# Where tiles start in SBUF: moving whole-row tiles from 128 bytes past a multiple of 256 to multiples of 1 KiB

## The chip, the cores and the metric

The kernel runs on one core of one Trainium2 chip; the program uses none of the others. The metric is the device time of one execution in microseconds (us), median of several.

## The reference, cut to what matters

`x` has the shape 8 x 4096 x 2112, float32, 276.8 MB. Each group of four consecutive rows has its mean taken off:

```python
x_r = x.reshape(B, S // 4, 4, D)
pooled = x_r.mean(axis=2)
upsampled = np.repeat(pooled, 4, axis=1)
return (x - upsampled).astype(np.float32)
```

Every byte has to be read from HBM once and written once; the page has 276.82 MB read and 276.82 MB written.

## The kernel before

One group of four rows is 8448 floats, 33792 bytes, and is put into one partition; 128 groups make a tile of 4.3 MB. There are 64 tiles. They lie in SBUF, the core's own memory; `x` and the output lie in HBM, the large memory. A load goes from HBM to SBUF, a store back. Loads are issued from the sync queue, stores from the scalar queue, and six buffers let them overlap.

```python
STRIDE = 4
IO_BUFS = 6
...
    W = STRIDE * D                                              # 8448
    xg = x.rearrange("b (g f) d -> (b g) (f d)", f=STRIDE)      # 8192 x 8448
    og = out.rearrange("b (g f) d -> (b g) (f d)", f=STRIDE)

    io_pool = ctx.enter_context(tc.tile_pool(name="io", bufs=IO_BUFS))
    sum_pool = ctx.enter_context(tc.tile_pool(name="sum", bufs=1))

    for g0 in range(0, G, P):
        gsz = min(P, G - g0)
        x_tile = io_pool.tile([P, W], mybir.dt.float32)
        nc.sync.dma_start(out=x_tile[:gsz], in_=xg[g0:g0 + gsz])          # load
        ...                                    # three tensor_add: s = sum of the four rows
        nc.vector.scalar_tensor_tensor(...)    # x_tile = s * (-1/4) + x_tile
        nc.scalar.dma_start(out=og[g0:g0 + gsz], in_=x_tile[:gsz])        # store
```

In the built program the first `x_tile` starts at byte 16512 of each partition, which is 64 x 256 + 128. A buffer is 33792 = 132 x 256 = 33 x 1024 bytes long, so all six start 128 bytes past a multiple of 256.

## Time and profile before

The median is 1286.44 us. What matters of the profile (a packet is one record of a DMA engine in the trace; a row packet moves one partition's 33792 bytes):

| what | value | view |
|---|---|---|
| span | 1284.7 us | page |
| VectorE (DVE) busy | 1026.1 us, 80% | page, busy times |
| DMA engines busy | 9 tenths or more in 39 of 40 slices | page, slices |
| loads and stores, share of the 16 engines' span | 50.0% and 49.9% | page, DMA queues |
| DVE waiting for loads | 237.3 us | waits |
| a row packet of 33792 bytes, recorded duration | 1251 ns, median of both queues | packet records in the trace |

These are lines of the page of the kernel before. "q1" carries the loads and "q10" the stores (packets, MB, share of 16 engines' span). In the slices each digit is the busy share of a fortieth of the span in tenths. In the groups of instructions the columns are: line, engine, operation, tiles, shapes, count, then busy us, mean ns of one, and idle time just before.

```profile
span 1284.7 us, 674 instructions
DVE 1026.1 (80%) x256; POOL 0.2 (0%) x4
...
DVE  5998778787787877878778787787887878778784
...
DMA  9999999999999999999999999999999999999998
...
q1 hardware_dynamic: 9216, 276.83, 50.0%
q10 hardware_dynamic: 9216, 276.83, 49.9%
...
L46 DVE SCALAR_TENSOR_TENSOR x_tile<-s,x_tile 128x8448 f32<-128x8448 f32 x64 | 573.3, 8958 | 2.2
L43 DVE TENSOR_TENSOR s<-x_tile 128x2112 f32<-128x2112 f32 x64 | 150.9, 2358 | 237.5 <-DMA x_tile<-in_x_dram 237.3
L45 DVE TENSOR_TENSOR s<-s,x_tile 128x2112 f32<-128x2112 f32 x128 | 301.8, 2358 | 4.4
```

The two queue shares add up to the whole span: the DMA engines have no slack. DVE has 20%, and it lies just where DVE waits for a load. The stretches view (busy times, granted clock, DMA share, GB/s) says the same of a short stretch and of the long middle:

```profile
core 0: us, DVE busy (x) POOL busy (x), PEclk, DMA share, GB/s
8.00:30.00 22.00, 16.81 (x5) 0.00 (x0) 1.00 1.00 433
100.00:1200.00 1100.00, 881.46 (x221) 0.00 (x0) 1.00 1.00 433
```

433 GB/s is the steady rate.

### The profile page before, as it was taken

Reading aid. Unit: us, or ns where it says so; the run is one execution under the profiler, and the core shown is the slowest. Engines: PE = TensorE matmul, PEld = TensorE weight load, DVE = VectorE, ACT = ScalarE, POOL = GpSimd, SP = SyncE. Lnnn points to the kernel's source line nnn. Section 1 sums busy time; section 2 is a strip of 40 time slices with the busy share of each in tenths; the row PEclk is TensorE's granted clock in tenths of the full one; section 3 lists DMA queues with packets and bytes.
Section 4 is the critical chain, followed back from the end, with each engine's and each line's share of the span. In section 5 each row is a group of like instructions: output and inputs, shape, how many; then the busy total and the mean of one; then the engine's idle time right before and its main releaser. Section 6 shows DMA issues by size and latency. Waiting matters only on the chain.

```text
span 1284.7 us, 674 instructions
## 1 busy us (share of the span) xinstructions
DVE 1026.1 (80%) x256; POOL 0.2 (0%) x4
## 2 busy tenths in 40 slices
DVE  5998778787787877878778787787887878778784
POOL 0000000000000000000000000000000000000000
DMA  9999999999999999999999999999999999999998
GB/s 404 421 438 438 433 425 437 438 427 432 437 437 426 435 437 431 429 437 437 431 428 438 437 431 429 437 436 432 428 438 436 430 430 437 437 426 433 438 431 380
DMA packets 18437, 553.70 MB, mean 431 GB/s; under 512 B 2048, under 2 KB 2048, under 8 KB 2048
## 3 DMA queue, kind: packets, MB, share of 16 engines
q1 hardware_dynamic: 9216, 276.83, 50.0%
q10 hardware_dynamic: 9216, 276.83, 49.9%
q14 instruction: 5, 0.04, 0.0%
HBM read 276.82 MB, written 276.82 MB: 431 GB/s over the span
## 4 chain that ended last, share of the span: by engine, by line
DVE 80%; another core or an unknown queue 17%; DMA 1%; issue 1%; DVEq 0%
DVE x_tile L46 45%; DVE s L45 24%; DVE s L43 12%; DMA x_tile<-in_x_dram 1%; DVEq L43 0%
## 5 line engine op out<-in xcount | busy, mean ns | idle before, releaser
L46 DVE SCALAR_TENSOR_TENSOR x_tile<-s,x_tile 128x8448 f32<-128x8448 f32 x64 | 573.3, 8958 | 2.2
L43 DVE TENSOR_TENSOR s<-x_tile 128x2112 f32<-128x2112 f32 x64 | 150.9, 2358 | 237.5 <-DMA x_tile<-in_x_dram 237.3
L45 DVE TENSOR_TENSOR s<-s,x_tile 128x2112 f32<-128x2112 f32 x128 | 301.8, 2358 | 4.4
L69 POOL MEMSET const-bfloat16-1.0<- 128x1 bf16 x1 | 0.1, 103 | 0.0
L69 POOL MEMSET const-uint8-127<- 128x1 uint8 x1 | 0.1, 102 | 0.0
L69 POOL MEMSET const-float32-0.0<- 128x1 f32 x1 | 0.1, 100 | 0.2 <-issue 0.2
L69 POOL MEMSET const-float32-1.0<- 128x1 f32 x1 | 0.1, 99 | 0.0
## 6 DMA issues: line engine op xcount, KB each, us to landing
x_tile<-in_x_dram SPq DMA_DIRECT2D x64, 4224.0 KB, 59.6
out_dram<-x_tile ACTq DMA_DIRECT2D x64, 4224.0 KB, 43.8
```

Source lines behind the costliest of these rows:

```text
L43: nc.vector.tensor_add(out=s[:gsz], in0=rows[:, 0, :], in1=rows[:, 1, :])
L45: nc.vector.tensor_add(out=s[:gsz], in0=s[:gsz], in1=rows[:, f, :])
L46: nc.vector.scalar_tensor_tensor(out=rows, in0=s[:gsz, None, :].to_broadcast([gsz, STRIDE, D]), scalar=-1.0 / STRIDE, in1=rows, op0=mybir. ...
L69: nc = _bacc.Bacc("TRN2", target_bir_lowering=False, num_devices=1)
```

## The change

The intent is to have every row start at an SBUF address that is a multiple of 1 KiB. That a start 128 bytes past a multiple of 256 costs each packet the time of 128 bytes (4 beats), 4.8 us in all, was the author's guess; no trace had shown it. A small tile that nobody uses is allocated first:

```diff
+PAD = 224
...
+    pad_pool = ctx.enter_context(tc.tile_pool(name="pad", bufs=1))
+    pad_pool.tile([P, PAD], mybir.dt.float32, name="pad")
     io_pool = ctx.enter_context(tc.tile_pool(name="io", bufs=IO_BUFS))
```

The 896 bytes move the first tile from 16512 to 17408 = 17 x 1024, and the other five with it. The instructions and their order on each engine stay the same. Here and in the recorded texts a beat is 32 bytes and a cycle 1.176 ns, the time of 32 bytes by the measured difference between packets of 33792 and of 768 bytes (1214.0 ns for 33024 bytes, at run768_aligned below). Both are units for reckoning; no run shows a clock or steps of that size. In these units the bytes of a row are 1056, and its recorded 1251 ns are 1063, 7 more.

## The prediction

> **What bounds the kernel now.** The DMA engines. The page shows a span of 1284.7 us, DVE busy 1026.1 us (80%), and DMA at 9 tenths in all but the last slice; the queue table gives the loads 50.0% and the stores 49.9% of the 16 engines' span. Each moves 276.83 MB as 8192 row packets of 33792 bytes (one partition row of a tile) and 1024 small ones. Share times span times 16 over 8192 gives 1.25 us a packet; the trace's packet records say it sharply: the median packet of either queue takes 1251 ns. An engine serves 2 x 8192 / 16 = 1024 row packets one after another: 1024 x 1.251 = 1281.0 us, leaving 5.4 us of the measured 1286.44 for start, end and a few slow packets. DVE's only large wait is 237.3 us for loads (the wait table). The chain of waits is 80% DVE work, but runs through queues that are never empty: DVE has 20% slack, DMA none.
>
> **What the change does.** It adds an unused 896-byte tile, so that the first x tile moves from byte 16512 of a partition (64 x 256 + 128) to 17408 (17 x 1024). A tile row is 33792 = 132 x 256 bytes, so all six buffers keep that alignment, and HBM rows keep theirs. The instruction order is the same. DVE operands move together and should keep their 8958 and 2358 ns.
>
> **What it is worth.** [...] All of it is critical: the engines are never idle. 1286.4 - 4.8 = 1281.6 us, 0.4%.
>
> The doubt: [...] a load writes SBUF and reads an HBM row that is aligned already. Yet load packets take the same 1251 ns. Either a write pays too, or the 7 cycles over 1056 are all fixed, and nothing is gained. I give the full gain 60%, stores alone 10%, nothing 25%. [...]
>
> **Predicted:** 1281.8 us, range 1279.5 to 1286.8 (8 in 10). Faster by over 2%: 0.02; within 2%: 0.97; slower: 0.01.
>
> **What would show it.** Median row packet of both queues 1246 ns in place of 1251 (1251 for loads only: writes don't pay; for both: no effect). Steady slices' GB/s up by about 0.4% (mean from 431 to 432 or 433). DVE's groups unchanged, its idle time before the first add 237 us down by about 5. DMA still at 9 tenths throughout.
>
> **What would make it wrong.** A fixed overhead instead of the 4 beats; another cost of alignment[...].

## The result, and the profile after

In the same rounds the kernel after took 1286.45 us (median of 6 runs, 1286.41 to 1286.58) and the kernel before 1286.48 us (6 runs, 1286.44 to 1287.14). The ratio is 0.9999, with a 95% interval of 0.9986 to 1.0012. Here and below a ratio is the mean time of one kernel's fast runs over the mean of the other's fast runs of the same rounds, so it is not quite the ratio of the medians. The 4.8 us that I gave a 60% chance did not come.

The lines of the page after that answer to those above:

```profile
span 1284.8 us, 674 instructions
DVE 1026.1 (80%) x256; POOL 0.2 (0%) x4
...
q1 hardware_dynamic: 9216, 276.83, 50.0%
q10 hardware_dynamic: 9216, 276.83, 49.9%
...
L49 DVE SCALAR_TENSOR_TENSOR x_tile<-s,x_tile 128x8448 f32<-128x8448 f32 x64 | 573.3, 8958 | 2.2
L46 DVE TENSOR_TENSOR s<-x_tile 128x2112 f32<-128x2112 f32 x64 | 150.9, 2358 | 237.6 <-DMA x_tile<-in_x_dram 237.3
L48 DVE TENSOR_TENSOR s<-s,x_tile 128x2112 f32<-128x2112 f32 x128 | 301.8, 2358 | 4.4
```

And the stretches view of the kernel after:

```profile
8.00:30.00 22.00, 16.74 (x5) 0.00 (x0) 1.00 1.00 432
100.00:1200.00 1100.00, 881.52 (x221) 0.00 (x0) 1.00 1.00 433
```

The same DVE durations, the same wait of 237.3 us, the same rate. The packet records agree: the median row packet takes 1251 ns in both queues, before and after.

One thing in the packet records is different from what I had read before. The *duration* of a packet is not its *pace*. I sorted the starts of the row packets between 200 and 1100 us and took every sixteenth, since 16 engines run side by side. The difference from one to the next is 1247 ns in 635 of 721 cases before and in 635 of 720 after, and 1247.9 ns on average in both (the average contains what the small packets cost: the page counts 2048 under 512 bytes, 16 for each of the 128 transfers). So recorded packets of one engine overlap by about 4 ns, and an engine finishes a row every 1247 ns, not every 1251. Of the 1286.4 us, 1024 x 1247.9 ns = 1277.8 us are rows, and some 8.6 us start and end. 1247 ns are 1060 cycles: the 1056 of the bytes and 4 more.

### The profile page after: what moved, and what is told of

It reads as the page before. It is cut to its first block, busy times and chain, and to the rows that moved or that the text cites. A ratio compares the mean times of both kernels' runs of the same rounds, so it can differ in the third digit from the quotient of the medians.

```text
span 1284.8 us, 674 instructions
## 1 busy us (share of the span) xinstructions
DVE 1026.1 (80%) x256; POOL 0.2 (0%) x4
## 2 busy tenths in 40 slices
DMA packets 18437, 553.70 MB, mean 431 GB/s; under 512 B 2048, under 2 KB 2048, under 8 KB 2048
## 4 chain that ended last, share of the span: by engine, by line
DVE 80%; another core or an unknown queue 17%; DMA 1%; issue 1%; DVEq 0%
DVE x_tile L49 45%; DVE s L48 24%; DVE s L46 12%; DMA x_tile<-in_x_dram 1%; DVEq L46 0%
## 5 line engine op out<-in xcount | busy, mean ns | idle before, releaser
L46 DVE TENSOR_TENSOR s<-x_tile 128x2112 f32<-128x2112 f32 x64 | 150.9, 2358 | 237.6 <-DMA x_tile<-in_x_dram 237.3
```

The lines of the kernel that those rows point to most:

```text
L46: nc.vector.tensor_add(out=s[:gsz], in0=rows[:, 0, :], in1=rows[:, 1, :])
```

## The experiments

Twelve kernels ran, in three calls. "Pace" is always the mean distance of packet starts on one engine (all starts in a stretch, times 16), from the packet records; the stretches view shows the same as GB/s. Three stretches are told apart in each run: the first 30 us or so, when only loads run because no tile is ready to be stored; the long middle, where loads and stores alternate (before, 32 loads and 32 stores start in each 5 us once the mix is steady); and the last 30 us or so, stores alone.

### First call: does a start off 256 cost anything at all?

To make a cost per packet large, rows are cut into runs of 768 bytes, 3 blocks of 256, each placed at its own 1 KiB step in SBUF. HBM stays contiguous. The results are still right.

```diff
-IO_BUFS = 6
+IO_BUFS = 4
+C = 192       # elements in one run of a row
+PITCH = 256   # elements from run to run in SBUF
+OFF = 0       # elements skipped before a run; 32 in run768_off128, 1 in run768_off4
...
-        x_tile = io_pool.tile([P, W], mybir.dt.float32)
-        nc.sync.dma_start(out=x_tile[:gsz], in_=xg[g0:g0 + gsz])
+        x_tile = io_pool.tile([P, W // C, PITCH], mybir.dt.float32)
+        data = x_tile[:gsz, :, OFF:OFF + C]
+        nc.sync.dma_start(out=data, in_=xg[g0:g0 + gsz].rearrange("p (n c) -> p n c", c=C))
...
```

The sums and the subtraction work on views of the same runs, one subtraction for each of the four rows; the pad of the change is kept, so that `OFF` alone sets the alignment.

The fourth kernel of the call is the kernel before with whole rows at 4 bytes past a multiple of 256:

```diff
+SKIP = 33   # from 128 bytes past a multiple of 256 to 4 bytes past one
...
-        x_tile = io_pool.tile([P, W], mybir.dt.float32)
+        x_wide = io_pool.tile([P, W + 64], mybir.dt.float32)
+        x_tile = x_wide[:, SKIP:SKIP + W]
```

**row_off4**

> Whole-row packets of 33792 bytes that start 4 bytes past a multiple of 256 in SBUF (before: 128 past; after: 0 past). Theory A, the start of a packet costs nothing and the 7 cycles over 1056 beats are paid at every address: row packets 1251 ns, time 1286.4 us. [...]

Measured: 1286.79 us, ratio to before 1.0002 (0.9986 to 1.0019); pace 1247 ns, median duration 1251 ns. Correct. A start 4 bytes past, which is not even a multiple of 32, costs nothing here either. (The later runs show that a mix hides a cost that one-way traffic has, 32.96 ns in the mix against 37.63 with loads alone for 768 bytes at 128 past, so this run says nothing of one-way traffic.)

**run768_aligned**

> Each row in 44 runs of 768 bytes, 1 KiB apart in SBUF, each at a multiple of 1 KiB; 45056 packets on an engine. It measures what a packet costs besides its bytes. [...] If instead the 1251 ns of a row is all rate (27.0 bytes a ns) and no packet overhead: 28.4 ns, about 1285 us. [...] it is the base of the next two.

Measured: 1494.05 us. The pace is 32.96 ns in the middle, more than the 28.4 ns expected without an overhead, and less than 7 cycles over the 24 beats would make it (31 cycles, 36.5 ns): my 7 cycles came from the recorded duration (36 ns here), not from the pace. From 768 to 33792 bytes the pace rises by 1247.0 - 32.96 = 1214.0 ns for 33024 bytes, which is 32 bytes in 1.1764 ns, or 27.2 bytes a ns on one engine: the cycle defined above. What remains of the 32.96 ns after 24 beats is 4.7 ns, 4 cycles. So the pace of both sizes is *bytes / 32 + 4* cycles a packet: 28 for 768 bytes, 1060 for a row.

The stretches view of run768_aligned shows loads alone, the mix, and stores alone, in this order:

```profile
10.00:30.00 20.00, 14.76 (x7) 0.00 (x0) 1.00 1.09 373
200.00:1200.00 1000.00, 698.17 (x301) 0.00 (x0) 1.00 1.09 373
1479.00:1487.00 8.00, 0.00 (x0) 0.00 (x0) 1.00 1.09 373
```

The DMA share of 1.09 is the overlap of recorded packets again (36 over 32.96 is 1.09). 373 GB/s throughout: aligned, the three stretches are alike.

**run768_off128**

> As run768_aligned, but each run starts 128 bytes past a multiple of 256 in SBUF. Theory A: same packet time and same total as run768_aligned within 1%. Theory B [...]: 4 beats more, 4.7 ns a packet, about 212 us more in all. [...]

Measured: 1499.68 us, 5.6 us or 0.4% more than run768_aligned, not 212. By its total theory A holds. But the same view says something else:

```profile
10.00:30.00 20.00, 12.72 (x6) 0.00 (x0) 1.00 1.09 326
200.00:1200.00 1000.00, 698.25 (x302) 0.00 (x0) 1.00 1.09 373
1484.00:1492.00 8.00, 0.00 (x0) 0.00 (x0) 1.00 1.04 327
```

With loads alone the rate is 326 in place of 373 GB/s, with stores alone 327; in the mix it is 373 as if the tiles were aligned. In the packet records the loads' pace is 37.63 ns against 32.95, exactly 32 cycles against 28. So an extra of the size in theory B, 4 cycles (4.7 ns), is there for these packets where traffic goes one way, and it vanishes where loads and stores alternate. Neither A nor B had this; the run was worth more by its stretches than by its time.

**run768_off4**

> As run768_aligned, but each run starts 4 bytes past a multiple of 256 in SBUF. Theory A: same as run768_aligned within 1%. Theory B: [...] 1 to 2 beats, 1.2 to 2.4 ns a packet, 50 to 110 us more. [...]

Measured: 1499.64 us, the same as run768_off128 within 0.04 us; 326 GB/s (37.65 ns, 32 cycles) with loads alone, 326 with stores alone, 373 in the mix. By its total theory A holds here too. 4 bytes and 128 bytes past cost the same, 4.7 ns more than aligned with loads alone, and not the 1.2 to 2.4 of theory B. What both runs share is that their 768 bytes touch four blocks of 256 bytes instead of three: four times 8 cycles (9.4 ns) is the 32 that both show.

### Second call: blocks or starts, and why is the mix spared?

The new theories are guesses from the paces of the first call: D (the cost belongs to an engine's reading or writing side and is averaged over loads and stores), E (it goes with the blocks touched in SBUF, and shows only while traffic goes one way), F (any start off 256 costs a fixed amount, whatever it touches). The first expectation has what each says in numbers.

Runs of 1408 bytes, 5.5 blocks, tell blocks from starts: 128 bytes past, they still touch 6 blocks; 192 bytes past, 7. The diff to run768_aligned:

```diff
-C = 192       # elements in one run of a row
-PITCH = 256   # elements from run to run in SBUF
+C = 352       # elements in one run of a row
+PITCH = 512   # elements from run to run in SBUF
-OFF = 0
+OFF = 0       # 32 in run1408_off128, 48 in run1408_off192
```

**run1408_off0**

> Each row in 24 runs of 1408 bytes (5.5 blocks of 256), 2 KiB apart in SBUF, at multiples of 2 KiB; 24576 packets on an engine. Theory D (sides): an engine spends beats + 4 cycles on a packet itself, and each of its two sides, the reading and the writing one, 8 cycles for each 256-byte block that the packet touches there; [...] over alternating loads and stores each side's mean counts, and the slowest of the three sets the pace. Here 44 + 4 = 48, sides 6 x 8 = 48: 48 cycles, 56.5 ns, about 1397 us. Theory E[...]: 48 cycles, 1397 us. Theory F (start): a side pays a fixed 8 cycles for any start off 256, not by blocks; half of the HBM runs start 128 past 256, so at the HBM side about 48 cycles as well: 1397 us.

Measured: 1398.90 us, pace 56.5 ns with loads alone and in the mix. The 4 cycles over the bytes are found at a third size: 44 + 4 = 48 cycles are 56.5 ns. (In the built program the runs start at 17408, which is 1 KiB past a multiple of 2 KiB, and not at multiples of 2 KiB; what the argument needs, a multiple of 256, holds.)

**run1408_off128**

> As run1408_off0, each run 128 bytes past a multiple of 256 in SBUF; it still touches 6 blocks. Theory D: no cost anywhere, 48 cycles in the loads-only start too, about 1397 us. Theory E with blocks: the same. Theory F: 52 cycles (61.2 ns) while only loads run, and in the mix (52 + 48) / 2 = 50 cycles, about 1455 us.

Measured: 1399.06 us; 56.46 ns with loads alone, 56.51 in the mix. These starts, 128 bytes off, touch no further block and cost nothing. Theory F falls.

**run1408_off192**

> As run1408_off0, each run 192 bytes past a multiple of 256 in SBUF; it touches 7 blocks. Theory D: 56 cycles (65.9 ns) while only loads run; in the mix (56 + 48) / 2 = 52 cycles, 61.2 ns, about 1512 us. Theory E: 65.9 ns while only loads run, but 48 cycles in the mix, about 1397 us. Theory F: as run1408_off128 (52 cycles loads only, about 1455 us).

Measured: 1404.41 us; 65.89 ns (56.0 cycles, 7 blocks x 8) with loads alone, 56.51 ns (48 cycles) in the mix. The stretches view of run1408_off128, then of run1408_off192:

```profile
10.00:30.00 20.00, 15.53 (x7) 0.00 (x0) 1.00 1.06 399
200.00:1200.00 1000.00, 746.51 (x322) 0.00 (x0) 1.00 1.06 399
```

```profile
10.00:30.00 20.00, 13.74 (x6) 0.00 (x0) 1.00 1.06 342
200.00:1200.00 1000.00, 746.57 (x323) 0.00 (x0) 1.00 1.06 399
```

With loads alone, that is, writes to SBUF, the seventh block costs 65.89 - 56.46 = 9.4 ns, 8 cycles. The last stretch of the same two runs shows it for stores, which read SBUF; run1408_off128 first, then run1408_off192:

```profile
1387.00:1395.00 8.00, 0.00 (x0) 0.00 (x0) 1.00 1.07 387
```

```profile
1391.00:1399.00 8.00, 0.00 (x0) 0.00 (x0) 1.00 1.02 342
```

342 GB/s are 65.9 ns, again 56 cycles for 7 blocks. This comes late: in the 11 us from 1369 us on, stores alone still ran at 388 GB/s. And at 6 blocks stores alone are a little slower than the mix, 383 GB/s (50 cycles) from 1370 to 1380 us, in run1408_off0 as in run1408_off128. Half of these runs start 128 bytes past a multiple of 256 in HBM, and the third call shows that such writes cost something (307 GB/s in place of 373 for 768 bytes).

Theory D said 52 cycles in the mix and some 1512 us; it got 48 cycles and 1404 us, so the averaging over an engine's sides falls in the form I gave it. E is left.

**hbm128_sbuf128.** Could D be saved by an HBM side that has slack? This kernel misaligns HBM too. It moves only the first 40 runs of each row, shifted by 128 bytes, and leaves the rest of the output untouched. Its output is wrong, which doesn't matter for the time. The diff to run768_off128:

```diff
+SHIFT = 32    # elements skipped at the start of a row in HBM
+USED = 40 * C   # a row's first 40 runs; the rest stays untouched
...
-        x_tile = io_pool.tile([P, W // C, PITCH], mybir.dt.float32)
+        x_tile = io_pool.tile([P, USED // C, PITCH], mybir.dt.float32)
...
-... in_=xg[g0:g0 + gsz].rearrange("p (n c) -> p n c", c=C))
+... in_=xg[g0:g0 + gsz, SHIFT:SHIFT + USED].rearrange("p (n c) -> p n c", c=C))
```

and the same for the store.

> Wrong result on purpose: 40 runs of 768 bytes of each row, which start 128 bytes past a multiple of 256 both in HBM and in SBUF; 40960 packets on an engine. SBUF alone off 128 cost nothing in the mix (28 cycles, 32.96 ns; here 1358 us). Theory D: now both sides touch 4 blocks in every packet, 32 cycles, 37.6 ns, about 1552 us. Theory E: 28 cycles in the mix, about 1360 us.

Measured: 1368.13 us, not 1552, and 8 us over E's 1360, which left out the two one-way stretches. In the mix 28.02 cycles; with loads alone 31.99; and with stores alone only 307 GB/s (768 x 16 / 307 = 40.0 ns, 34 cycles). If one writing side of an engine had to take the loads' 32 and the stores' 34 cycles in turn, the mix could not be faster than 33. It runs at 28. D is out in any form in which loads and stores pay these costs in turn.

### Third call: the cost at the size of a row, and two rivals of E

**loads_aligned and loads_off128** are the kernels after and before with their 64 loads and the sums, but one store, of the last tile. Their outputs are wrong, which doesn't matter for the times. With almost all traffic one way, E says that the alignment of the change is worth what I had predicted for it, halved because the stores are gone.

```diff
-        nc.vector.scalar_tensor_tensor(...)
-        nc.scalar.dma_start(out=og[g0:g0 + gsz], in_=x_tile[:gsz])
+        if g0 + P >= G:     # loads and sums alone; one store, of the last tile
+            nc.scalar.dma_start(out=og[g0:g0 + gsz], in_=x_tile[:gsz])
```

> Wrong result on purpose: the kernel after, with its 64 loads of whole rows and the sums, but with one store, of the last tile. Almost all traffic writes SBUF. 520 row packets on an engine at 1060 cycles (1247 ns): all theories say some 670 us, and a steady 1247 ns from packet to packet. It is the base of loads_off128.

> The same from the kernel before: rows start 128 bytes past a multiple of 256 in SBUF. Theory E (the SBUF side takes 8 cycles for each 256-byte block touched, in one direction): 133 blocks, 1064 cycles against the engine's 1060, so 1251.8 ns from packet to packet in place of 1247, and 2.4 us more than loads_aligned (0.35%). Theory H, a long packet never pays (the extra is a matter of short packets): the same time as loads_aligned within 0.5 us.

Measured: 657.40 us aligned (4 runs, 657.32 to 657.49) and 659.80 us at 128 past (4 runs, 659.62 to 659.96). The difference is 2.4 us, as E has it, and the runs don't overlap; the base itself came out 13 us under my rough 670. The stretches view of loads_aligned, then of loads_off128, shows first loads and then the middle:

```profile
10.00:30.00 20.00, 13.72 (x6) 0.00 (x0) 1.00 1.01 436
100.00:600.00 500.00, 353.37 (x151) 0.00 (x0) 1.00 1.00 433
```

```profile
10.00:30.00 20.00, 13.81 (x6) 0.00 (x0) 1.00 1.00 433
100.00:600.00 500.00, 351.45 (x150) 0.00 (x0) 1.00 1.00 432
```

That view is too coarse for 0.4%; the packet records have it. Aligned, the pace is 1247.8 ns throughout (small packets included). At 128 past it is also 1247.8 ns for about the first 40 packets of an engine (the gap after the very first one left out), and from the hundredth on 1251.6 to 1252.2, as means of 100 or 200 packets. 133 blocks x 8 cycles = 1064 cycles = 1251.8 ns. So the extra does not show for a while and then does, by these records some 3.9 ns a packet of the 4.7 that E has. Theory H falls. This fits with the loads-only start of the kernel before, which shows nothing: it is some 25 packets long on each engine, and its pace is 1247 ns before and after.

**loads768_off128_2q** has only loads, in 768-byte runs at 128 past, issued in turn from both queues, with one store at the end (wrong, like the two above). Of the diff to run768_off128, the part with the queues:

```diff
-        nc.sync.dma_start(out=data, ...)
+        queue = nc.sync if g0 // P % 2 == 0 else nc.scalar
+        queue.dma_start(out=data, ...)
```

> Wrong result on purpose: loads alone, in runs of 768 bytes at 128 past a multiple of 256 in SBUF, issued in turn from two queues; 22528 load packets on an engine. With one queue of loads such a packet took 32 cycles (37.6 ns), in a mix of loads and stores 28 (32.96 ns). Theory E (direction: the SBUF write side is used by every packet): 32 cycles, 37.6 ns, some 880 us. Theory G (a queue alone pays, and a second queue fills its gaps, whatever the direction): 28 cycles, 32.96 ns, some 770 us.

Measured: 870.93 us. The pace is 37.65 ns, 32.0 cycles, from the start to the end. Its stretches view and its queues:

```profile
10.00:30.00 20.00, 1.65 (x1) 0.00 (x0) 1.00 1.09 326
100.00:600.00 500.00, 268.80 (x114) 0.00 (x0) 1.00 1.09 326
```

```profile
q10 hardware_dynamic: 186384, 142.74, 54.5%
q1 hardware_dynamic: 180736, 138.41, 54.0%
```

Each queue carries half of the loads (q10 the one store besides), and the rate stays at 326 GB/s. A second queue does not hide the cost (326 GB/s); a second direction does (373 in the mix of run768_off128). Theory G falls.

**hbm128_sbuf0** is hbm128_sbuf128 with `OFF = 0`: misaligned in HBM alone.

> Wrong result on purpose: 40 runs of 768 bytes of each row, 128 bytes past a multiple of 256 in HBM alone, aligned in SBUF. If an HBM read pays by blocks as SBUF does: 32 cycles (37.6 ns) while only loads run; if it does not: 28 cycles (32.96 ns). In the mix 28 cycles either way, about 1362 us, 5 us less than hbm128_sbuf128 if the loads-only start pays nothing.

Measured: 1365.00 us, 3.1 us less than hbm128_sbuf128 (5 were expected). The stretches view of hbm128_sbuf128, then of hbm128_sbuf0, each with loads alone, the mix, and stores alone:

```profile
8.00:28.00 20.00, 12.98 (x7) 0.00 (x0) 1.00 1.09 326
200.00:1200.00 1000.00, 702.60 (x332) 0.00 (x0) 1.00 1.09 373
1332.00:1354.00 22.00, 14.51 (x7) 0.00 (x0) 1.00 1.09 307
```

```profile
8.00:28.00 20.00, 14.30 (x7) 0.00 (x0) 1.00 1.09 373
200.00:1200.00 1000.00, 697.67 (x330) 0.00 (x0) 1.00 1.09 373
1332.00:1354.00 22.00, 9.63 (x5) 0.00 (x0) 1.00 1.10 307
```

Reads from HBM at 128 past cost nothing (373 GB/s); writes to HBM at 128 past do when stores run alone (307, against 373 in run768_aligned). In the mix, again, nothing (373).

### The runs together

Cycles are ns / 1.1764. The middle columns are worked out from bytes and addresses, the last two are measured paces.

| packets | start past 256 in SBUF | SBUF blocks touched | beats + 4 | blocks x 8 | loads alone | mix |
|---|---|---|---|---|---|---|
| 768 B | 0 | 3 | 28 | 24 | 32.95 ns, 28.0 | 32.96 ns, 28.0 |
| 768 B | 128 | 4 | 28 | 32 | 37.63 ns, 32.0 | 32.96 ns, 28.0 |
| 768 B | 4 | 4 | 28 | 32 | 37.65 ns, 32.0 | 32.96 ns, 28.0 |
| 1408 B | 0 | 6 | 48 | 48 | 56.49 ns, 48.0 | 56.51 ns, 48.0 |
| 1408 B | 128 | 6 | 48 | 48 | 56.46 ns, 48.0 | 56.51 ns, 48.0 |
| 1408 B | 192 | 7 | 48 | 56 | 65.89 ns, 56.0 | 56.51 ns, 48.0 |
| row (after) | 0 | 132 | 1060 | 1056 | 1247.8 ns | 1247.9 ns |
| row (before) | 128 | 133 | 1060 | 1064 | 1251.7 ns, later on | 1247.9 ns |

With loads alone the pace is in each row the larger of the two middle columns. In the mix it is always the first of them. The row lines contain the small packets.

What fits the pace of loads alone and of the mix in all twelve runs is this. In the mix a packet takes beats + 4 cycles: 32.96, 56.51 and 1247 ns for 768, 1408 and 33792 bytes. With loads alone it takes 8 cycles for each 256-byte block that it touches in SBUF, where that is more: 37.63 ns for 4 blocks and 65.89 ns for 7 are 9.41 ns a block, and the row's 1251.7 ns for 133, later on, are the same. (Of block sizes in powers of two only 256 fits: in blocks of 128 bytes or less, or of 512 or more, 768 bytes at 128 past touch no more of them than aligned ones, and they took 4.7 ns longer.) A guess at why the mix is spared, drawn from these paces alone and shown by no run: when loads and stores alternate, SBUF is written by only every second packet and read by every second one; if the block cost is counted for each direction by itself, each has two packets' time, 2 x 1060 cycles for rows, for one packet's 1064. The extra block of the kernel before would fit into that easily. What was measured is that to remove it gained nothing (1286.45 against 1286.48 us).

What is shown is the dependence on direction, on blocks, and not on the queue. That each direction is counted by itself is the inference; what in the hardware does so, no run tells. The fit has no rule for writes to HBM, which took 34 cycles for 768 bytes at 128 past when stores ran alone; nor does it say why stores show the SBUF cost later than loads (388 GB/s for 11 us and then 342 in run1408_off192). Whole rows one way were tried with loads, not with stores. I also ran no kernel with many loads to a store: by that guess (an estimate from 32 and 28 cycles) the mix of 768-byte packets would begin to pay when loads are more than 28/32 = 7/8 of the packets.

No version that beats both kernels came out of this. The middle runs at 1060 cycles a row for 1056 beats, 1247 ns; by the measured 27.2 bytes a ns (an estimate from the paces of 768 and 33792 bytes) 1242 of them go with the bytes.

## Why the prediction was right or wrong

- *The DMA engines bound the kernel, DVE has slack.* Right: DVE durations and waits are unchanged, and all kernels with other packet sizes followed the packets' pace (1286 us at 1060 cycles a row, 1494 us at 28 cycles for 768 bytes).
- *The time stays within 2%, between 1279.5 and 1286.8 us.* Right: 1286.45 us. This was luck as far as the mechanism goes: the range held because it contained the case of no effect, which I gave 25%, and for another reason than the runs showed (a fixed overhead of 7 cycles). The low odds of a larger gain were the author's estimate. The point, 1281.8 us, was 4.65 us too low.
- *The 4.8 us.* This is the step that failed, in two ways. The estimate took the recorded 1251 ns, 7 cycles over the 1056 of the bytes, for a packet's time, and 4 of the 7 for the cost of its start; no trace showed that share. First, 1251 ns is a packet's recorded duration; the pace is 1247 ns, 1060 cycles. Had I taken the distance of starts, the 1251 ns would have been found 4 ns too high for a misaligned row before anything ran. Second, the cost of a misaligned start was added to the overhead. With loads alone the pace is the larger of two counts, and the one by blocks was seen only in one-way traffic (37.63 ns, against 32.96 in the mix, in run768_off128). Even with loads alone the sum fails: for 1408 bytes at 128 past it gives 44 + 4 + 4 = 52 cycles, and they took 48.
- *"All of it is critical: the engines are never idle."* Wrong in its reason. The engines are never idle, and still taking the extra block away gained nothing (1286.45 against 1286.48 us). Why is not shown; the guess above is that the block is counted for each direction by itself, and half of the packets go each way.
- *"Either a write pays too, or the 7 cycles over 1056 are all fixed, and nothing is gained."* The doubt was the right one. Writes to SBUF do pay, as reads of it do (326 and 327 GB/s in run768_off128), but not in a mix (373). The fixed part is 4 cycles, not 7.
- *What the alignment is worth.* The 4 cycles per misaligned packet were the right size for a row in a kernel that only loads (2.4 us over the 512 load packets of each engine in loads_off128, 4.7 ns each). As a rule they were not: 1408 bytes paid nothing at 128 past and 8 cycles at 192 past.

## What to carry to other kernels

Read the pace of a saturated DMA stream from the distance of packet starts, not from a packet's recorded duration; the two differ by 9% for 768-byte packets here. In these runs, aligning SBUF tiles to 256 bytes mattered only in stretches in which transfers went one way, and then by the blocks touched (14% for 768-byte runs, 0.4% for whole rows of 33 KiB); while loads and stores alternated it gained nothing (373 GB/s at 0, 4 and 128 past; 433 for whole rows). Before costing a saving at full, ask whether the resource it frees is the one that sets the pace: "always busy" (here 9 tenths or more in 39 of 40 slices, and 0.03 us gained) names the engine, not each thing that the engine waits on.
